# A hybrid recurrence step on one core: a limit on TensorE's instructions in time, joins in halves, small weights on ScalarE's queue, lent operand tiles as raw buffers

## The chip, the cores and the metric

The kernel runs on one core of a Trainium2 chip. The metric is the device time of one launch in microseconds, as the median of several runs.

## What is computed

One layer of a model that mixes two recurrences, for 128 context tokens and 512 sample tokens, all in float32 (D = 2048, FFN width 5632):

```python
h = rms_norm(x, L['norm_mix_pre']) * (1.0 + scale_m) + shift_m
proj = h @ L['w_in']                                  # 2048 x 5408
xl, gl, pr = jnp.split(proj, [LRU_WIDTH, 2 * LRU_WIDTH], axis=-1)
# RG-LRU, forward and backward: gates by 8 heads of 128x128, then a linear scan
lru_out = ((hs_f + hs_b) * jax.nn.gelu(gl)).astype(dt)
# RWKV-7, forward and backward, 16 heads of 64: S = S*w + (S @ -kk)(kk*a) + v k, y = S r
rwkv_out, wkv_fin = rwkv7(pr, shift_fn, wkv_S0, L)
out = jnp.concatenate([lru_out, rwkv_out], axis=-1) @ L['w_out']
x = x + gate_m * rms_norm(out, L['norm_mix_post'])
h = rms_norm(x, L['norm_ffn_pre']) * (1.0 + scale_f) + shift_f
gate, up = jnp.split(h @ L['ffn_w_gu'], 2, axis=-1)
x = x + gate_f * rms_norm((jax.nn.silu(gate) * up) @ L['ffn_w_down'], L['norm_ffn_post'])
```

The six shifts, scales and gates are 2048 wide each and come from `silu(c) @ w_mod + b_mod`.

## The kernel before

All 640 tokens lie in the free dimension, as two halves of 320; channels lie in the partitions, 128 a tile. A projection's weights arrive as raw tiles of 128x512 floats (256 KB) and are split into a high and a low part in a rounded format (`split`, tile w, six buffers); a product is then three full-width matmuls of the rounded kind for each half of the tokens (tile ps). The normalized input lies split in 16 pairs of tiles, hi0 to hi15 and lo0 to lo15. When the input projection `w_in` has read a pair for the last time, the pair is free until the mixer's result k is loaded back from DRAM (`mixd`) into pair k by `mix_load`.

The program text is not written in the order in which the engines run it. Each part of the work is a Python generator, a stream with a priority. The class `Sched` keeps a planned clock for each engine, knows a planned duration for each instruction and delay for each DMA, and takes, one after the other, the stream whose next instructions could start earliest (`run`). A stream that yields a list of instructions has them issued together. So the order on every engine is fixed when the program is built, and each engine works it off in that order; SyncE's queue of DMAs too. The planner's numbers change only this order.

Streams in the mixer, all at once: `loader` fetches raw weights, first of w_in, then of the output projection `w_out`, and mixes in raw tiles of `w_mod` (`mod_rate`); `main` multiplies (lowest priority, so it fills TensorE's idle time); `lru` does the RG-LRU for 8 pairs of heads, two directions each, with weights lruw; `gates` uses the same tile for the weights gup; `elem` prepares the 16 jobs (8 head pairs, two directions) of RWKV-7 with weights up; `inverse` and `join` invert each job's triangular 64x64 blocks; `chain` runs the recurrence over the chunks; `gn` normalizes and stores the result.

A `join` inverts by blocks: ten chunks, two heads. It sends 40 matmuls of 32x32 tiles from jt and af in one list, an evacuation by ScalarE into yj, 40 matmuls of 32x16 from yj, an update by VectorE, and then two lists of 20. A plain float32 matmul counts as two matmul records and two weight loads in the trace; the rounded kind as one of each.

The output projection comes in two passes over the 16 output tiles: the first (`EARLY`) takes the operand tiles 0 to 3 and 8 to 11 and goes on while the mixer still works; `evac_part` copies each partial sum into the only gt tile and stores it (`opd`). The second (`LATE`) takes the rest and adds the partial sums. Then follow the residual, which has VectorE busy, and the FFN, which keeps TensorE busy to the end.

Raw tiles come from one pool of four buffers (`self.raws`, `free_raw`) until the first pass is done. SyncE issues every DMA. In the profile nearly all compute instructions stand under line 127 and DMAs under line 121, in a helper that builds instructions; so tiles tell where one belongs. pa and pc are the accumulators of the mixer's small work.

Of the kernel before, what the change touches and what calls it, by code (L numbers as in the profile page):

```python
# [11 lines left out]
F32 = mybir.dt.float32  # L12
# [13 lines left out]
T = TP + TS  # L26
# [8 lines left out]
NC = 10  # L35
# [12 lines left out]
PATIENCE = 1.5  # L48
MODE, HOLD, HOLD_MOD = 0.35, 0.0, 8.0
LAT = {  # L50
    "pe": {"pe": 0.0, "act": 0.2, "dve": 0.2, "pool": 0.2, "sync": 0.15},
# [54 lines left out]
class Eng:  # L106
# [3 lines left out]
    def __getattr__(self, op):  # L110
        f, eng = getattr(self._r, op), self._n

        def make(*args, **kw):
# [3 lines left out]
            if op == "dma_start":  # L117
                n = 4
                for s in out.shape:
                    n *= s  # L120
                return Op(eng, lambda: f(*args, **kw), _box(out), [_box(x) for x in ins], 0.48, None, n)  # L121
            aset = None
# [62 lines left out]


class Sched:

# [5 lines left out]
    def __init__(self):  # L194
# [9 lines left out]
        self.now = 0.0  # L204
        self.win, self.busy, self.slow, self.parts, self.mode = 0, 0.0, True, [], True

    def own(self, tile_, res, t):
# [82 lines left out]
    def emit(self, op):  # L290
# [14 lines left out]
        if op.bytes:  # L305
            self.bus = max(e, self.bus) + op.bytes / 330e3
            e, eng = self.bus + 1.4, "dma"
            self.lane[self.ndma % 8] = e
            self.ndma += 1
# [53 lines left out]
    def run(self, until=None):  # L363
        while self.streams and not (until is not None and until in self.ev):
            best = None
            cand = []
            for st in self.streams:
# [13 lines left out]
                if ops[0].eng == "pe" and whole(ops[0]) != self.mode and (  # L381
                        self.mode is False or self.now - st[4] < (HOLD if st[0] < 8 else HOLD_MOD)):
                    s += MODE
                cand.append((s, st, ops))
                if best is None or s < best[0]:
# [8 lines left out]
            for op in best[2]:  # L394
                self.emit(op)
            self.step(best[1], None)
            self.poll()

    def fire(self, *names):
# [27 lines left out]
class Step:  # L427
# [223 lines left out]
    def free_raw(self):  # L651
        return next((r.take() for r in self.raws if r.slots), None)

# [172 lines left out]
    def loader(self):  # L826
# [41 lines left out]
        mk = [("m", k) for k in range(KT)]  # L868
        self.mod_rate = MOD_RATE2
        for m in range(KT):  # L870
            yield from self.rows(a["w_out"][m], self.evac_part(m), mk, EARLY)
# [33 lines left out]
    def lru(self):  # L905
        sc = self.sc
        for q in range(NPAIR):
# [5 lines left out]
            for d in range(2):  # L913
                r, av, i = yield self.take("u", 3)
                wt = yield self.take("lruw")
                yield self.q.dma_start(wt, self.a["lruw"][q, d])

# [62 lines left out]
    def elem(self):  # L980
        sc = self.sc
        for n in range(NJ):
# [7 lines left out]
            up = yield self.take("up")  # L990
            yield self.q.dma_start(up, self.a["lup"][p, d])
            sw, av, cs, pd = yield self.take("t", 4)
# [97 lines left out]
    def join(self, n):  # L1090
# [7 lines left out]
        for h in range(2):  # L1098
            for e in range(4):
                p0, c0 = 64 * h + 16 * e, 16 * (e % 2)  # L1100
                yield self.q.dma_start(got[p0:p0 + 16, :, c0:c0 + 16], self.xsc[p % 2][d][h, e].rearrange("c k i -> k c i"))
        yield self.v.transpose(out=turned, in_=got)
        Q = [slice(32 * q, 32 * q + 32) for q in range(4)]
        p3 = lambda t, w: t[:, 0:NC * w].rearrange("p (c t) -> p c t", t=w)
        ps = yield self.take("pa")
        yield [self.mm(ps[r, c * 32:(c + 1) * 32], af[r, c, 0, q // 2, 32 * (q % 2):32 * (q % 2) + 32], tq[r, c, :])
               for c in range(NC) for q, r in enumerate(Q)]
        yield self.copy(yy, p3(ps, 32))
        sc.rel(ps)
        o = slice(16, 32) if d == 0 else slice(0, 16)  # L1110
        ps = yield self.take("pa")
        yield [self.mm(ps[r, c * 16:(c + 1) * 16], yy[r, c, :], xd[r, c, o]) for c in range(NC) for r in Q]
        yield self.stt(xd[:, :, o], p3(ps, 16), self.rmask[:, d:d + 1], xd[:, :, o])
# [151 lines left out]
    def gates(self):  # L1265
# [3 lines left out]
        for p in range(NPAIR):  # L1269
            gw = yield self.take("lruw")  # L1270
            g1, g2 = gw[:, 0], gw[:, 1]
            yield self.q.dma_start(g1, self.a["gup1"][p])
            yield self.q.dma_start(g2[0:32], self.a["gup2"][p])
            g = yield self.take("gt")
# [56 lines left out]
    def evac_part(self, m):  # L1331
        def go(acc):
            t = yield self.take("gt")
            yield self.copy(self.v2(t), acc.v)
# [703 lines left out]
```

## Time and profile before

| | |
|---|---|
| three runs | 3404.69, 3408.0, 3411.7 us; median 3408.0 |
| profiled execution | 3410.4 us, span 3408.6 us |
| TensorE busy | 3213.6 us (94%), 25068 matmuls and as many weight loads |
| VectorE, ScalarE, GpSimd busy | 2205.9 us (65%), 1541.9 us (45%), 1465.0 us (43%) |
| stages | input norm to 100 us; mixer and input projection to about 1255 us; output projection to 1590 us; residual to 1700 us; FFN to the end |
| mean granted clock of TensorE | 0.966 |

All times are from one profiled execution. PE is TensorE, PEld its weight loads, DVE VectorE, ACT ScalarE, POOL GpSimd, SP SyncE; a small q stands for an engine's sequencer. A row of the windows view gives start and end, the length, the busy time of PE, PEld, DVE, ACT and POOL with the number of instructions, then the granted share of TensorE's clock (1.00 is 2.4 GHz, 0.50 is 1.2 GHz), the DMA engines' share and GB/s. A row of the waits view names who waited for whom, the total in us, how often, and the longest. A row of the timeline gives the start and the length in us of a group of instructions of one kind, what it writes and reads, how many, and in brackets the idle time before it with what ended it; "issue" is a wait that nothing in the profile explains.

### The profile page before, as it was taken

Reading aid. Unit: us, or ns where it says so; the run is one execution under the profiler, and the core shown is the slowest. Engines: PE = TensorE matmul, PEld = TensorE weight load, DVE = VectorE, ACT = ScalarE, POOL = GpSimd, SP = SyncE. Lnnn points to the kernel's source line nnn. Section 1 sums busy time; section 2 is a strip of 40 time slices with the busy share of each in tenths; the row PEclk is TensorE's granted clock in tenths of the full one; section 3 lists DMA queues with packets and bytes.
Section 4 is the critical chain, followed back from the end, with each engine's and each line's share of the span. In section 5 each row is a group of like instructions: output and inputs, shape, how many; then the busy total and the mean of one; then the engine's idle time right before and its main releaser. Section 6 shows DMA issues by size and latency. Waiting matters only on the chain.

```text
span 3408.6 us, 67001 instructions
## 1 busy us (share of the span) xinstructions
PE 3213.6 (94%) x25068; PEld 2892.3 (85%) x25068; DVE 2205.9 (65%) x3878; ACT 1541.9 (45%) x3282; POOL 1465.0 (43%) x1736
## 2 busy tenths in 40 slices
PE   6899999999999989897699999999999999999997
PEld 4787888888888877786499999999999988888885
DVE  4465667776776762267988888888888862323324
ACT  4435456665666656243444444444444432312223
POOL 1353345444544453256666666566666640000001
PEclk9999989999999999997799999999999999999998
DMA  9533334433333354685533333333333342423323
GB/s 382 173 100 93 98 91 115 111 97 110 99 91 109 104 162 145 205 277 173 176 103 95 103 103 98 96 101 102 91 106 100 101 147 77 136 77 105 97 77 133
DMA packets 262774, 422.55 MB, mean 124 GB/s; under 512 B 74801, under 2 KB 87729, under 8 KB 258353
## 3 DMA queue, kind: packets, MB, share of 16 engines
q1 hardware_dynamic: 262448, 418.27, 40.3%
q8 instruction: 198, 3.24, 0.4%
q14 instruction: 128, 1.04, 0.1%
HBM read 365.19 MB, written 52.96 MB: 123 GB/s over the span
## 4 chain that ended last, share of the span: by engine, by line
PE 80%; DVE 9%; DMA 6%; issue 2%; ACT 2%; SPq 1%; POOL 1%; DVEq 0%; POOLq 0%; ACTq 0%
PE pb L127 41%; PE ps L127 19%; PE pc L127 11%; PE pa L127 6%; DMA raw<-in_w_out_dram 2%; PE pm L127 2%; DVE pr L127 1%; DVE x L127 1%; DVE o L127 1%; SPq L121 1%; DVE lo L127 1%; DMA raw<-in_wmod_dram 1%; DVE xl L127 1%; DVE hi L127 1%; DVE u L127 1%
## 5 line engine op out<-in xcount | busy, mean ns | idle before, releaser
L127 PE MATMUL ps<-hi,w 128*128 128x320 f32 x3712 | 937.1, 330 | 34.4 <-POOL w L127 17.9
L127 PEld LDWEIGHTS ps<-hi,w 128*128 128x128 f32 x3712 | 649.3, 195 | 78.3 <-POOL w L127 26.7
L127 PE MATMUL ps<-lo,w 128*128 128x320 f32 x1856 | 600.5, 329 | 2.0 <-DVE lo L127 1.9
L127 POOL TENSOR_SCALAR w<-raw 128x256 fp32r<-128x256 f32 x403 | 196.4, 487 | 679.6 <-PE ps L127 475.6
L127 POOL TENSOR_TENSOR w<-raw,w 128x256 fp32r<-128x256 f32 x500 | 414.2, 830 | 159.8 <-PE ps L127 72.6
L127 POOL TENSOR_TENSOR hi<-raw 128x256 f32<-128x256 f32 (+1 forms) x307 | 291.6, 966 | 208.1 <-PE pb L127 188.4
L127 PEld LDWEIGHTS ps<-lo,w 128*128 128x128 f32 x1856 | 360.9, 194 | 18.9 <-issue 8.3
L127 ACT ACTIVATE w<-raw 128x256 fp32r<-128x256 f32 x421 | 173.7, 413 | 374.1 <-PE pb L127 259.7
L127 POOL TENSOR_TENSOR lo<-raw 128x256 f32<-128x256 f32 (+1 forms) x260 | 241.7, 943 | 171.6 <-PE pb L127 107.3
L127 PE MATMUL pb<-hi,lo 128*128 128x320 f32 (+1 forms) x984 | 292.4, 339 | 0.0
L127 DVE TENSOR_TENSOR w<-raw,w 128x256 fp32r<-128x256 f32 x324 | 187.0, 578 | 89.4 <-ACT w L127 77.5
L127 PE MATMUL pb<-hi,hi 128*128 128x320 f32 (+1 forms) x740 | 225.1, 340 | 0.6 <-DVE hi L127 0.6
L127 PE MATMUL pb<-lo,lo 128*128 128x512 f32 (+1 forms) x646 | 204.3, 356 | 0.0
L127 PEld LDWEIGHTS pb<-hi,lo 128*128 128x128 f32 x984 | 179.6, 189 | 13.3
L127 PE MATMUL pb<-lo,hi 128*128 128x320 f32 (+1 forms) x604 | 189.9, 346 | 0.0
L127 PE MATMUL pb<-x,lo 128*128 128x320 f32 x774 | 172.0, 310 | 2.7 <-DVE x L127 2.1
L127 PE MATMUL pb<-o,hi 128*128 128x320 f32 x726 | 173.8, 309 | 0.0
L127 PE MATMUL pb<-o,w 128*128 128x320 f32 x792 | 160.8, 311 | 0.4 <-DVE w L127 0.4
L127 DVE TENSOR_TENSOR lo<-raw 128x256 f32<-128x256 f32 (+1 forms) x268 | 157.3, 611 | 0.0
L127 PE MATMUL pb<-x,hi 128*128 128x320 f32 x590 | 154.5, 311 | 2.3 <-DVE hi L127 2.3
L127 ACT ACT_TABLE_LOAD x115 | 147.5, 1283 | 6.8 <-DMA st<-in_cT_dram 2.5
L127 DVE TENSOR_TENSOR hi<-raw 128x256 f32<-128x256 f32 (+1 forms) x221 | 145.6, 681 | 0.0
(395 smaller groups left out, 7504.7 us busy)
## 6 DMA issues: line engine op xcount, KB each, us to landing
raw<-in_w_gu_dram SPq DMA_DIRECT2D x352, 256.0 KB, 2.6
raw<-in_wmod_dram SPq DMA_DIRECT2D x256, 256.0 KB, 3.7
raw<-in_w_dn_dram SPq DMA_DIRECT2D x176, 256.0 KB, 2.6
raw<-in_w_in_dram SPq DMA_DIRECT2D x160, 256.0 KB, 3.4
mraw<-in_wmod_dram SPq DMA_DIRECT2D x32, 1024.0 KB, 8.8
raw<-in_w_out_dram SPq DMA_DIRECT2D x64, 256.0 KB, 4.3
gud<-z SPq DMA_DIRECT2D x44, 320.0 KB, 2.5
x<-in_xT_dram SPq DMA_DIRECT2D x32, 320.0 KB, 5.5
```

Source lines behind the costliest of these rows:

```text
L121: return Op(eng, lambda: f(*args, **kw), _box(out), [_box(x) for x in ins], 0.48, None, n)
L127: o = Op(eng, lambda: f(*args, **kw), _box(out), [_box(x) for x in ins], _cost(eng, op, out, ins), aset, 0)
```

## The change

The planner gets three new numbers. `AT_ONCE`, `FETCH` and `LATE_FETCH`: where TensorE's next list would bring the count of its instructions (two for a rounded matmul or a transpose, four for a plain one) within 2.6 us over 300, the list is planned 2.5 us later, so that another stream's work goes first. A DMA's planned landing is later by up to 1.0 us, by its size. A DMA issued by an engine other than SyncE is planned at 0.1 us of that engine. The first two lists of a join are yielded in two halves of 20. The loads of lruw, gup and up (48 in all) go from SyncE's queue (`self.q`) to ScalarE's (`self.s`). From the moment when the loader turns to w_out (`away`) until the last RG-LRU result is stored (`("mix", 7)`), `free_raw` may also take hi13 to hi15 and lo13 to lo15, six tiles more, and `evac_part` one of hi7, lo7, hi12 and lo12 instead of gt.

```diff
+FETCH, AT_ONCE, LATE_FETCH = 2.6, 300, 2.5
@@ Eng
-                return Op(eng, lambda: f(*args, **kw), _box(out), [_box(x) for x in ins], 0.48, None, n)
+                return Op(eng, lambda: f(*args, **kw), _box(out), [_box(x) for x in ins], 0.48 if eng == "sync" else 0.1, None, n)
...
+def count(ops):
+
+    return sum(2 if op.cost in (0.115, 0.147, 0.227) else 4 for op in ops)
@@ Sched.emit
-            e, eng = self.bus + 1.4, "dma"
+            e, eng = self.bus + 1.4 + min(1.0, op.bytes / 256e3), "dma"
@@ Sched.run
+                if ops[0].eng == "pe" and self.recent(s) + count(ops) > AT_ONCE:
+                    s += LATE_FETCH
...
+            if eng == "pe":
+                self.hist.append((self.now, count(best[2])))
...
+    def recent(self, t):
+
+        while self.hist and self.hist[0][0] < self.clk["pe"] - FETCH:
+            self.hist.popleft()
+        return sum(n for e, n in self.hist if e > t - FETCH)
@@ Step
     def free_raw(self):
-        return next((r.take() for r in self.raws if r.slots), None)
+        return next((r.take() for r in self.raws if r.slots), None) or self.lend(13, 14, 15, n=512)
+
+    def lend(self, *ks, n=T):
+
+        if "away" in self.sc.ev and ("mix", 7) not in self.sc.ev:
+            for k in ks:
+                for tag in ("hi%d" % k, "lo%d" % k):
+                    if self.R[tag].slots:
+                        return self.R[tag].take().bitcast(F32)[:, 0:n]
+        return None
@@ loader
         self.mod_rate = MOD_RATE2
+        self.sc.fire("away")
@@ lru
-                yield self.q.dma_start(wt, self.a["lruw"][q, d])
+                yield self.s.dma_start(wt, self.a["lruw"][q, d])
@@ elem
-            yield self.q.dma_start(up, self.a["lup"][p, d])
+            yield self.s.dma_start(up, self.a["lup"][p, d])
@@ join
+        halves = range(NC // 2), range(NC // 2, NC)
...
-        yield [self.mm(ps[r, c * 32:(c + 1) * 32], af[r, c, 0, q // 2, 32 * (q % 2):32 * (q % 2) + 32], tq[r, c, :])
-               for c in range(NC) for q, r in enumerate(Q)]
+        for cs in halves:
+            yield [self.mm(ps[r, c * 32:(c + 1) * 32], af[r, c, 0, q // 2, 32 * (q % 2):32 * (q % 2) + 32], tq[r, c, :])
+                   for c in cs for q, r in enumerate(Q)]
...
-        yield [self.mm(ps[r, c * 16:(c + 1) * 16], yy[r, c, :], xd[r, c, o]) for c in range(NC) for r in Q]
+        for cs in halves:
+            yield [self.mm(ps[r, c * 16:(c + 1) * 16], yy[r, c, :], xd[r, c, o]) for c in cs for r in Q]
@@ gates
-            yield self.q.dma_start(g1, self.a["gup1"][p])
-            yield self.q.dma_start(g2[0:32], self.a["gup2"][p])
+            yield self.s.dma_start(g1, self.a["gup1"][p])
+            yield self.s.dma_start(g2[0:32], self.a["gup2"][p])
@@ evac_part
-            t = yield self.take("gt")
+            t = yield lambda: self.lend(7, 12) or (self.R["gt"].take() if self.R["gt"].slots else None)
```

The order changes nearly everywhere, since one new number in the planner shifts all that follows. Three places show how.

TensorE at the seventh of the 16 joins, before: the first batch (jt,af), full-width matmuls of the input projection (ps), the second batch (jt,yj).

```order
L127 MATMUL pa<-jt,af 32x32 x40
L127 MATMUL ps<-hi_1165,w 128x320
L127 MATMUL ps<-lo_1166,w 128x320
L127 MATMUL ps<-hi_1165,w 128x320
L127 MATMUL ps<-lo_1166,w 128x320
L127 MATMUL ps<-hi_1165,w 128x320 x2
L127 MATMUL ps<-hi_1234,w 128x320
L127 MATMUL ps<-lo_1235,w 128x320
L127 MATMUL ps<-hi_1234,w 128x320
L127 MATMUL ps<-lo_1235,w 128x320
L127 MATMUL ps<-hi_1234,w 128x320
L127 MATMUL pa<-jt,yj 32x16 x40
```

The same join in the new order (pm are the modulation's matmuls):

```order
L128 MATMUL pa<-jt,af 32x32 x40
L128 MATMUL pm<-raw,scv 32x256 x4
L128 MATMUL ps<-hi_967,w 128x320
L128 MATMUL ps<-hi_1029,w 128x320
L128 MATMUL ps<-lo_1030,w 128x320
L128 MATMUL pa<-jt,yj 32x16 x20
L128 MATMUL ps<-hi_1029,w 128x320
L128 MATMUL pa<-jt,yj 32x16 x20
```

The first batch is still whole; the second is cut, with one full-width matmul between its halves, and eleven matmuls between the batches have become seven.

SyncE's queue around the second load of lruw, the one issued at 493.03 us, before: kd is the store of a k tile that waits to be computed.

```order
L121 DMA raw<-in_w_in_dram 128x512
L121 DMA raw<-in_wmod_dram 128x512
L121 DMA raw<-in_w_in_dram 128x512
L121 DMA kd_5132<-gt 128x640
L121 DMA lruw<-in_lruw_dram 128x256
```

ScalarE's queue around the first load of lruw in the new order, with what each row waits for (DMAHW are landings of earlier DMAs):

```order
L122 DMA up<-in_lup_dram 128x128 [waits DMAHW7_49]
L128 ACT_TABLE_LOAD
L128 ACTIVATE t<-pa,c_rp 128x320 [waits PE_49] x4
L128 ACTIVATE gt<-ps,c_lp 128x640 [waits DMAHW3_49,DVE_49]
L128 ACTIVATE yj<-pa 128x320 [waits PE_49]
L122 DMA lruw<-in_lruw_dram 128x256 [waits DMAHW6_49,DMAHW1_49]
L128 ACT_TABLE_LOAD
```

The load no longer stands behind raw tiles and the store; it stands behind ScalarE's evacuation of a join's batch, and what follows on ScalarE stands behind it. Of the 48 loads, 43 carry a wait of the DMAHW kind.

SyncE's queue in the first pass of the output projection, before:

```order
L121 DMA raw<-in_w_out_dram 128x512
L121 DMA opd_80<-gt 128x640
L121 DMA raw<-in_wmod_dram 128x512
L121 DMA out_o_wkv_dram<-yy 128x64
L121 DMA raw<-in_wmod_dram 128x512
L121 DMA raw<-in_w_out_dram 128x512
```

The same place in the new order:

```order
L122 DMA raw<-in_w_out_dram 128x512
L122 DMA raw<-in_wmod_dram 128x512 x2
L122 DMA hi_16658<-in_w_out_dram 128x512
L122 DMA hi_16664<-in_wmod_dram 128x512
L122 DMA opd_80<-hi_16682 128x640
L122 DMA out_o_wkv_dram<-yy 128x64
```

Weights now also land in hi and lo tiles, and the partial sum leaves from one.

## Rows read from the trace of the kernel before

**Rows 1.** Windows by stage: busy time of each engine, granted clock, DMA share:

```profile
100.00:1255.00 1155.00, 1095.69 (x11570) 960.94 (x11571) 777.27 (x1641) 666.24 (x1608) 542.81 (x760) 0.96 0.38 107
...
1700.00:3409.00 1709.00, 1678.02 (x10010) 1569.92 (x10008) 1132.77 (x1783) 637.18 (x1171) 698.79 (x719) 0.99 0.34 103
```

**Rows 2.** TensorE's own waits, 100 to 1255 us: total us, times, longest:

```profile
PE pa L127 <- issue: 12.0, 7, 3.0
...
PE pa L127 <- DMA lruw<-in_lruw_dram: 6.4, 4, 2.5
...
PE pa L127 <- DMA lruw<-in_gup_dram: 3.4, 4, 1.1
...
PE ps L127 <- issue: 2.1, 1, 2.1
...
PE pa L127 <- DMA up<-in_lup_dram: 1.4, 2, 0.7
```

**Rows 3.** Timeline of TensorE in three places with join batches:

```profile
423.74 0.41 PE L127 MATMUL ps<-hi,w 128*128 128x320 f32 x1
423.99 0.30 PE L127 MATMUL ps<-lo,w 128*128 128x320 f32 x1
424.13 0.46 PE L127 MATMUL ps<-hi,w 128*128 128x320 f32 x2
...
553.67 0.89 PE L127 MATMUL pa<-jt,af 32*32 32x32 f32 x80
...
556.66 0.97 PE L127 MATMUL pa<-jt,yj 32*32 32x16 f32 x80
...
845.93 0.92 PE L127 MATMUL pa<-jt,af 32*32 32x32 f32 x80
...
847.95 0.69 PE L127 MATMUL pa<-jt,yj 32*32 32x16 f32 x60
851.31 0.51 PE L127 MATMUL pa<-jt,yj 32*32 32x16 f32 x20 [2.67 <-issue]
```

**Rows 4.** DMA queues, 848.7 to 851.3 us: packets, MB, share of 16 engines:

```profile
q8 instruction: 1, 0.02, 2.3%
```

**Rows 5.** Windows over half-clock stretches, columns as in rows 1; sums last:

```profile
850.70:860.90 10.20, 9.59 (x87) 8.76 (x87) 5.89 (x10) 5.76 (x8) 2.43 (x3) 0.50 0.10 28
...
sum 27.10, PE 25.15 PEld 21.28 DVE 8.73 ACT 12.64 POOL 5.11; mean PE 8.38 PEld 7.09 DVE 2.91 ACT 4.21 POOL 1.70
...
sum 13.30, PE 13.30 PEld 11.78 DVE 2.54 ACT 8.19 POOL 3.46; mean PE 6.65 PEld 5.89 DVE 1.27 ACT 4.09 POOL 1.73
...
1355.90:1362.60 6.70, 5.36 (x16) 4.57 (x17) 1.06 (x1) 3.88 (x7) 2.97 (x5) 0.50 0.59 186
...
sum 23.60, PE 16.81 PEld 15.54 DVE 4.30 ACT 7.44 POOL 6.11; mean PE 4.20 PEld 3.89 DVE 1.07 ACT 1.86 POOL 1.53
```

**Rows 6.** Chain from 490 us; issues of lruw; SyncE's waits, 100 to 1440 us:

```profile
493.03 4.79 DMA lruw<-in_lruw_dram
...
L121 SPq DMA_DIRECT2D lruw<-in_lruw_dram x16: 422/432/1656, 431.0 to 1345.2; - x16
...
SPq L121 <- DMA xsc<-xl: 14.1, 10, 2.9
```

**Rows 7.** Waits of TensorE, 1245 to 1372 and 1372 to 1440 us, and GpSimd's:

```profile
PE ps L127 <- POOL w L127: 6.9, 5, 3.9
...
PE ps L127 <- POOL w L127: 8.2, 7, 4.1
...
POOL w L127 <- DMA raw<-in_w_out_dram: 94.0, 23, 8.9
```

**Rows 8.** Issues of stores and loads by tile: ns min/median/max, first, last start:

```profile
L121 SPq DMA_DIRECT2D mixd<-y x8: 319/324/433, 391.3 to 1383.4; - x8
L121 SPq DMA_DIRECT2D mixd<-lh x8: 319/323/382, 556.4 to 1371.8; - x8
...
L121 SPq DMA_DIRECT2D opd<-gt x16: 326/417/454, 1234.0 to 1430.3; - x16
```

More of the change, by code (lines that the diff above doesn't have):

```diff
@@ L205, in __init__ @@
         self.win, self.busy, self.slow, self.parts, self.mode = 0, 0.0, True, [], True
+        self.hist = deque()
     def own(self, tile_, res, t):
```

## The prediction

> **What bounds the kernel now.** I read the windows by stage first, then TensorE's own waits, then single places in the timeline, and last the chain and the waits of the queue that issues DMAs. In the mixer's stretch, 100 to 1255 us, TensorE is busy 1095.69 of 1155 us, and after 1700 us it is busy 1678.02 of 1709 [rows 1]. TensorE is the bound in both, and since the change neither adds nor removes a matmul, time can be won only where TensorE waits or runs at its lower clock. After 1700 us there is next to nothing to win. So the whole forecast lies in the mixer and in the first pass of the output projection behind it.
>
> Three causes of lost time can be named there.
>
> First, the joins. A join sends a batch of 40 tiny matmuls (160 TensorE instructions: the timeline counts 80 matmul records and there are as many weight loads), some full-width ones, and a second batch of 40. In [rows 3] a second batch stops after 60 of its 80 records for 2.67 us with "issue" as the cause: no semaphore ends that wait. In just those 2.6 us one packet of the queue "instruction" moved [rows 4]. So I read it as TensorE's sequencer running out of fetched instructions. The waits view has 12.0 us of it on pa in 7 waits and one of 2.1 us on ps [rows 2]: 14.1 us. The granted clock then falls to 0.50, which is 1.2 GHz, the lower of the two levels: 850.7 to 860.9 us is the stretch behind the stall of [rows 3], and three such stretches (the others 359.2 to 369.4 and 1041.9 to 1048.6 us) add up to 27.1 us [rows 5]. Half of that is lost: 13.6 us. The joins cost 14.1 + 13.6 = 27.7 us at most.
>
> Second, the small weights (lruw, up). TensorE waits for them 6.4 + 3.4 + 1.4 = 11.2 us [rows 2]. The load at 493.03 us takes 4.79 us until TensorE goes on, and SyncE, which issues it, spends 422 to 1656 ns on an issue [rows 6]; it had to get past a store of k that waited for its data. Two half-clock stretches follow such waits (499.2 to 509.3 and 1134.1 to 1137.3 us), 13.3 us [rows 5], half of it 6.7. Together 17.9 us.
>
> Third, the first pass of the output projection. Up to the last linear-recurrence result, stored at 1371.8 us [rows 8], TensorE waits 6.9 us for split weights, and another 8.2 us until 1440 us [rows 7]. GpSimd, which splits them, waited 94.0 us for the raw weights' transfers in the same stretch [rows 7]. So four raw buffers are too few there. Four half-clock stretches add 23.6 us [rows 5], of which 11.8 are lost; the second of them ends at 1362.6 us, and it and the first are 6.7 us long, so 6.7 is lost up to 1372 and 5.1 behind. So 13.6 us within reach of the lent buffers and 13.3 us behind them, 26.9 in all.
>
> **The change part by part.**
>
> *Joins.* In the new order of TensorE 9 of the 16 joins have one of their first two batches cut in two, and the number of other matmuls from the first batch to the end of the second has risen in the median from 6.5 to 9. What that is worth is read from distance: a second batch that starts 2.02 us behind the first stalls for 2.67 us, while one that starts 2.99 us behind, at 556.66 us, goes through without a break [rows 3]. Two and a half full-width matmuls at 0.14 us (423.99 to 424.13 us [rows 3]) are 0.35 us, about a third of the distance between those two cases. The limit is also soft, and 7 joins stay whole. So of the 27.7 us I take four tenths, 11.1 us; the bounds are nothing and all. Against it stands the price of the cuts. The first full-width matmul behind a batch holds the array for 0.25 us (423.74 to 423.99 us) where 0.14 is usual [rows 3], and I allow as much on entering: 0.2 us a cut, 9 cuts, 1.8 us. Net 9.3 us.
>
> *Small weights.* 48 loads leave SyncE, where they stood in one row with weight loads that wait for a free buffer, and now stand on ScalarE behind whatever it does. Their issue takes 48 times 0.43 us, the median of SyncE's [rows 6], some 21 us of ScalarE, which is busy only 666.24 of these 1155 us [rows 1]; as long as that cover holds the price is nothing. The planner now also reckons with a later landing, so TensorE's matmuls that need the weights stand further behind. Nothing in the trace shows a load issued by ScalarE. The gain lies between nothing and 17.9 us; I take six tenths, 10.7, since the place shown in the order has the load behind an evacuation that itself waits for a join.
>
> *Lent tiles.* Six idle operand halves become raw buffers from the end of the input projection's loads until 1371.8 us, in the old time. Four buffers gave waits of 13.6 us there; ten should take away two thirds of that, 9.1 us. Behind it only the head start helps: a fifth of 13.3, 2.7 us. 11.8 us; bounds nothing and 26.9. The staging tiles for the partial sums cost nothing and hide a store that no engine on the path waits for.
>
> *What is late next.* A shorter filler could meet the recurrence. The last of its results is stored at 1383.4 us, the last partial sum at 1430.3 us [rows 8]: 46.9 us of cover, more than the sum below. In the new order the last normalizing matmul stands 43 projection matmuls further back, about 6 us at 0.14; the cover holds.
>
> *The sum.* 9.3 + 10.7 + 11.8 = 31.8 us. The profiled execution took 3410.4 us, 1.8 more than its span, and the median of the timed runs is 2.4 lower. 3410.4 - 31.8 - 2.4 = **3376 us**.
>
> **A rule that speaks against it.** The trace shows instruction packets inside the stalls. By the Trainium skill, page "Runtime: NRT & Kernel Launch", section "Instruction fetch mechanics", an engine's sequencer fetches the next block of instructions by itself while it works on the current one, and the cost of a block's end is mostly hidden. By that rule a limit on instructions in time has nothing to win. The stop in the midst of a batch, where no operand is new, and the packet in it speak against the word "mostly" here.
>
> **The rivals.**
>
> *The joins are bound by something else.* The stalls stay and only the cuts are paid: 3410.4 + 1.8 - 10.7 - 11.8 - 2.4 = 3387 us. For it: "issue" is only the name for what the profile can't tell. Against it: the packets [rows 4]. That result is the one that the Trainium skill's rule above would give.
>
> *The change doesn't do what it says.* The limit lets through 300 instructions where a join alone has 320, so stalls merely move, and the lent buffers fill early without help, since a split also needs one of six tiles for its halves. Then only the small weights pay: 3410.4 + 1.8 - 10.7 - 2.4 = 3399 us. For it: the seventh join in the order stands closer together than before. Against it: GpSimd's 94.0 us [rows 7].
>
> *All of it goes.* 3410.4 + 1.8 - 27.7 - 17.9 - 26.9 - 2.4 = 3337 us. Against it: a new order brings waits of its own.
>
> *Slower: ScalarE is held up by its own loads.* Of the 48 loads 43 carry a wait for the landing of an earlier DMA. On SyncE such a wait for a small store took 14.1 us in 10 cases, 1.4 us each [rows 6]. On ScalarE everything queues behind it: the recurrence's copies (yy, svu), for which TensorE waits in a fixed order. 43 x 1.4 = 60 us of ScalarE. If three quarters reach TensorE, that is 45 against the 31.8 gained: 3410.4 - 31.8 + 45 - 2.4 = 3421 us. From 53% on the kernel is slower than before. Against it: ScalarE has 489 us to spare, and at issue most landings lie well back.
>
> **How the numbers follow.** About 0.2% (6.8 us) is what a measurement here can tell from no change: 3401 to 3415 us is "same". The forecast has 0.42 (3360 to 3390 us). The rule's rival has 0.08, "all of it" 0.10: both faster. "Doesn't do what it says" has 0.24, of which 0.14 below 3401, 0.09 within and 0.01 above. ScalarE's rival has 0.16: 0.15 slower and 0.01 within. So faster 0.42 + 0.08 + 0.10 + 0.14 = 0.74, same 0.10, slower 0.16. The range reaches from 3342, which leaves out half of "all of it" (0.05), to 3411, which leaves out ScalarE's rival (0.15).
>
> **What would show it.** Right: in TensorE's waits between 100 us and the end of the input projection "issue" on pa falls from 12.0 to about 7 us, and waits for lruw and up from 11.2 to under 5; half-clock stretches behind joins get fewer; between the end of the input projection and the last recurrence store TensorE waits under 3 us for split weights; the stretch from the residual on keeps its length. Wrong: "issue" stays or moves to other tiles; ScalarE's waits grow around its loads and TensorE's waits for ScalarE with them; the first pass waits for GpSimd itself rather than for transfers. If the last part grows in length, the cause lies in a part of the order that I took as unchanged.

## The result

| | before | after |
|---|---|---|
| median of the runs | 3406.35 us (3400.58 to 3411.7) | 3356.6 us (3342.8 to 3366.87) |
| ratio, 95% interval | | 0.9852 [0.9809, 0.9894] |
| profiled execution, span | 3410.4, 3408.6 us | 3366.87, 3364.9 us |

The kernel became 50 us faster by the medians, 36 to 65 us by the interval. The forecast was 3376 us in a range of 3342 to 3411. The profiled execution of after is the slowest of its four, so its span shows 43.7 of the 50 us.

To see where they went I cut the execution at two points that every version has: SyncE's first issue of a w_out load and its last issue of opd. In each part I add up TensorE's **lost time** from its records: the gaps in which it neither multiplies nor loads weights, plus, for each stretch at the lower clock, its length times one minus the granted clock. The span less all lost time is 3097.0 us before and 3096.7 after (the first 100 us and the 24.2 us behind TensorE's last instruction counted as lost too, 24.2 in both). So lost time tells the difference where the lengths of the parts do not, since TensorE's work moves between them.

| lost time, us (idle + clock) | before | after | difference | predicted |
|---|---|---|---|---|
| mixer, from 100 us to the first w_out load | 51.4 + 41.0 = 92.4 | 46.0 + 32.4 = 78.4 | -14.0 | -20.0 |
| first pass, to the last opd | 27.8 + 17.1 = 44.9 | 6.9 + 10.2 = 17.1 | -27.8 | -11.8 |
| all behind it | 59.5 + 58.0 = 117.5 | 54.8 + 59.1 = 113.9 | -3.6 | 0 |

**The mixer.** TensorE's waits after, from 100 to 1255 us (who waited for whom; total us, times, longest), beside [rows 2]:

```profile
PE pc L128 <- DVE svu L128: 8.6, 13, 2.7
...
PE pc L128 <- issue: 5.1, 2, 2.7
...
PE pa L128 <- issue: 3.2, 5, 0.9
...
PE pa L128 <- DMA up<-in_lup_dram: 1.4, 4, 0.4
...
PE ps L128 <- issue: 1.0, 1, 1.0
...
PE pa L128 <- DMA lruw<-in_lruw_dram: 0.5, 1, 0.5
```

The small weights are nearly gone from the list: 1.4 + 0.5 = 1.9 us instead of 11.2. Their issue on ScalarE's queue (columns as in [rows 6]):

```profile
L122 ACTq DMA_DIRECT2D lruw<-in_lruw_dram x16: 334/335/364, 430.1 to 1329.3; - x16
```

"Issue" on pa fell from 12.0 to 3.2 us, but pc now has 5.1 us that it did not have; with ps the sum went from 14.1 to 9.3 us. One of the two pc stalls in the timeline of TensorE (start, length in us, idle time in brackets):

```profile
776.67 0.53 PE L128 MATMUL pa<-jt,yj 32*32 32x16 f32 x40
777.12 0.80 PE L128 MATMUL pc<-af,svu 128*64 128x64 f32 x20
777.86 0.79 PE L128 MATMUL pc<-ar,sa 64*64 64x64 f32 x18
781.36 0.47 PE L128 MATMUL pc<-ar,sa 64*64 64x64 f32 x2 [2.72 <-issue]
```

The join's half stands directly ahead of the recurrence's own two batches of 20 records each. The third batch stops after 18 of 20 for 2.72 us, as the join's did in [rows 3]. The queue "instruction" from 778.6 to 781.4 us (packets, MB, share of the engines), and the window from the end of the stall (columns as in [rows 1]):

```profile
q8 instruction: 1, 0.02, 2.2%
```

```profile
781.13:787.96 6.83, 6.60 (x130) 5.07 (x132) 3.01 (x6) 0.98 (x2) 0.00 (x0) 0.50 0.69 201
```

Again one packet, and then 6.83 us at half clock. So the same kind of stall came back at another batch, one that now follows directly on the cut join's half.

**The first pass.** The windows from the first w_out load to the last opd, before and then after:

```profile
1186.50:1430.30 243.80, 215.80 (x2053) 183.49 (x2052) 100.03 (x189) 129.03 (x287) 96.15 (x128) 0.93 0.54 160
```

```profile
1172.00:1391.10 219.10, 211.95 (x2091) 186.79 (x2092) 104.98 (x194) 120.27 (x274) 107.66 (x156) 0.95 0.60 182
```

About the same number of matmuls in 219.10 us instead of 243.80, with 182 GB/s instead of 160. The waits that have to do with the split weights w, in these windows, before:

```profile
POOL w L127 <- DMA raw<-in_w_out_dram: 89.5, 22, 8.9
...
PE ps L127 <- POOL w L127: 15.2, 12, 4.1
```

and after:

```profile
POOL w L128 <- PE ps L128: 81.5, 70, 5.4
...
POOL w L128 <- DMA raw<-in_w_out_dram: 3.4, 1, 3.4
```

GpSimd's wait for raw weights fell from 89.5 to 3.4 us. It now waits 81.5 us for TensorE to free a split tile, so the order of who waits has turned round, and TensorE's matmuls have no row for GpSimd's w left. The stores of the last partial sums (ns, first and last start), beside [rows 8]:

```profile
L122 SPq DMA_DIRECT2D mixd<-y x8: 326/380/624, 393.0 to 1368.6; - x8
```

```profile
L122 SPq DMA_DIRECT2D opd<-hi x12: 319/326/431, 1229.9 to 1358.4; - x12
L122 SPq DMA_DIRECT2D opd<-gt x4: 320/320/382, 1365.3 to 1391.1; - x4
```

From the last mixd<-y to the last opd there were 46.9 us of cover; now 22.5 are left (1391.1 - 1368.6).

### The profile page after: what moved, and what is told of

Read it like the earlier page. It is cut to its first block, busy times and chain, and to the rows that moved or that the text cites. A ratio compares the mean times of both kernels' runs of the same rounds, so it can differ in the third digit from the quotient of the medians.

```text
span 3364.9 us, 66999 instructions
## 1 busy us (share of the span) xinstructions
PE 3200.5 (95%) x25068; PEld 2888.0 (86%) x25068; DVE 2211.7 (66%) x3872; ACT 1532.3 (46%) x3265; POOL 1475.9 (44%) x1762
## 4 chain that ended last, share of the span: by engine, by line
PE 82%; DVE 9%; DMA 4%; ACT 2%; issue 2%; SPq 1%; POOL 1%; DVEq 0%; ACTq 0%; POOLq 0%
PE pb L128 43%; PE ps L128 20%; PE pc L128 12%; PE pa L128 6%; PE pm L128 2%; DVE pr L128 1%; DVE x L128 1%; DVE o L128 1%; DVE xl L128 1%; DVE bk L128 1%; DVE lo L128 1%; SPq L122 1%; DVE svu L128 1%; DMA raw<-in_w_in_dram 1%; DVE z L128 0%
## 5 line engine op out<-in xcount | busy, mean ns | idle before, releaser
L128 PE MATMUL ps<-hi,w 128*128 128x320 f32 x3712 | 919.7, 326 | 19.4 <-ACT hi L128 8.5
L128 POOL TENSOR_TENSOR w<-raw,w 128x256 fp32r<-128x256 f32 x469 | 388.7, 829 | 138.6 <-PE ps L128 56.5
L128 PEld LDWEIGHTS ps<-lo,w 128*128 128x128 f32 x1856 | 355.9, 192 | 20.5 <-issue 9.8
L128 PE MATMUL pb<-lo,lo 128*128 128x320 f32 (+1 forms) x932 | 282.5, 340 | 0.1
L128 PE MATMUL pb<-lo,hi 128*128 128x320 f32 (+1 forms) x695 | 211.2, 344 | 0.2 <-DVE lo L128 0.2
L128 DVE TENSOR_TENSOR hi<-raw,lo 128x512 fp32r<-128x512 f32 x88 | 60.9, 692 | 213.5 <-ACT lo L128 185.8
L128 PE MATMUL pb<-x,hi 128*128 128x320 f32 x936 | 197.7, 311 | 0.0
L128 DVE TENSOR_TENSOR lo<-raw,hi 128x512 fp32r<-128x512 f32 x85 | 58.9, 693 | 200.0 <-ACT hi L128 162.0
L128 PEld LDWEIGHTS pb<-lo,lo 128*128 128x128 f32 x932 | 167.8, 188 | 13.6 <-DVE z L128 0.3
L128 DVE TENSOR_TENSOR hi<-raw 128x128 f32<-128x128 f32 (+1 forms) x228 | 159.0, 712 | 0.0
L128 PEld LDWEIGHTS pb<-x,hi 128*128 128x128 f32 x936 | 154.2, 190 | 0.0
```

The source lines that it names most:

```text
L128: o = Op(eng, lambda: f(*args, **kw), _box(out), [_box(x) for x in ins], _cost(eng, op, out, ins), aset, 0)
```

## The experiments

Twelve more kernels were measured, in three groups of four, each group on one chip. A ratio stands against runs of before from the same group (medians 3400.72, 3399.65 and 3409.6 us); it is taken over the runs and is not the quotient of the two medians. "Bursts" counts TensorE's stalls of over 0.4 us, 100 to 1400 us, whose matmul has no releaser and that begin behind 250 or more TensorE instructions in 5 us.

| kernel | us | ratio [95%] | lost: mixer | first pass | behind | bursts |
|---|---|---|---|---|---|---|
| before | | 1 | 92.4 | 44.9 | 117.5 | 8, 14.9 us |
| lend_only | 3368.2 | 0.9887 [0.986, 0.9915] | 81.1 | 18.3 | 109.0 | 9, 17.9 |
| limit_only | 3386.29 | 0.994 [0.9919, 0.9961] | 56.4 | 41.8 | 109.7 | 3, 5.2 |
| weights_only | 3408.75 | 1.0017 [0.9996, 1.0038] | 97.6 | 50.0 | 105.1 | 3, 4.2 |
| landing_only | 3391.99 | 0.9976 [0.9956, 0.9996] | 78.0 | 47.8 | 111.3 | 8, 9.1 |
| after | 3356.6 | 0.9852 [0.9809, 0.9894] | 78.4 | 17.1 | 113.9 | 7, 9.0 |
| after_no_lend | 3378.56 | 0.9935 [0.9914, 0.9956] | 68.9 | 40.0 | 111.6 | 5, 5.5 |
| after_no_limit | 3371.35 | 0.9906 [0.9878, 0.9935] | 82.8 | 27.1 | 107.0 | 4, 5.8 |
| after_weights_sync | 3404.49 | 1.0012 [0.9997, 1.0026] | 122.5 | 21.1 | 106.8 | 2, 3.0 |
| after_no_landing | 3383.14 | 0.9941 [0.992, 0.9962] | 87.3 | 22.0 | 112.9 | 2, 3.0 |
| queue_before | 3398.64 | 0.997 [0.9953, 0.9987] | 77.5 | 46.0 | 117.7 | 9, 14.5 |
| queue_after | 3352.98 | 0.9848 [0.9817, 0.9878] | 77.9 | 12.8 | 115.2 | 7, 8.7 |
| shuffle_after | 3351.39 | 0.984 [0.9816, 0.9863] | 61.8 | 25.1 | 103.0 | 4, 8.3 |
| window5 | 3341.41 | 0.9809 [0.9792, 0.9827] | 54.4 | 4.2 | 106.6 | 0 |

The lost times are of one profiled execution each. How far those scatter shows in three kernels whose order on TensorE is the same to the row up to the loader's turn to w_out: before, lend_only and queue_before have 92.4, 81.1 and 77.5 us in the mixer. So differences of some 15 us there can be the execution and not the kernel. The same holds for a single wait: TensorE waits 11.2 us for lruw, gup and up in before and 4.2 + 1.6 + 1.2 = 7.0 in lend_only, where these loads stand as they stood. The span less all lost time lies between 3094.8 and 3103.1 us, except in limit_only (3114.0) and window5 (3113.4). The first theories were these. "First pass": the lent tiles are most of the gain. "Fetch": the limit ends the stalls at joins. "Truer order": the later planned landing removes the waits for small weights. "Shuffle": each new order moves the time either way, and the parts do not add up.

### The lent tiles: alone, and taken out

lend_only is the kernel before with these lines; after_no_lend is after without them:

```diff
-        return next((r.take() for r in self.raws if r.slots), None)
+        return next((r.take() for r in self.raws if r.slots), None) or self.lend(13, 14, 15, n=512)
+        self.sc.fire("away")
-            t = yield self.take("gt")
+            t = yield lambda: self.lend(7, 12) or (self.R["gt"].take() if self.R["gt"].slots else None)
```

> The kernel before with the lent tiles alone (six operand tiles as raw buffers, four as staging tiles in the first pass of the output projection). Theory 'first pass': TensorE's waits for split weights there (15.1 us) and the half-clock stretches behind them (11.8 us lost) are most of the 50 us that the change won; so about 25 us faster than before, 3381 us, and the last partial sum stored some 25 us earlier behind an unchanged mixer. Theory 'fetch': most was won at the joins; then this run is within 10 us of before. Theory 'shuffle': each new order moves the time by some 10 to 15 us either way and the parts don't add up.

> The changed kernel without the lent tiles. Theory 'first pass': it loses about 25 us, 3381 us, and the waits for split weights between the end of the input projection and the last partial sum are back at 10 us or more. Theory 'fetch' or 'shuffle': it loses under 10 us.

Alone the tiles give 0.9887 [0.986, 0.9915], some 38 us (32.5 by the medians); without them 28 us of the gain are missing (0.9935 - 0.9852 = 0.0083 of 3400). In the first pass of after_no_lend the waits are back: GpSimd waits 88.1 us for raw weights of w_out, and TensorE 15.9 for split ones. The window of lend_only from the first w_out load to the last opd:

```profile
1178.90:1388.70 209.80, 199.80 (x2034) 175.71 (x2035) 101.54 (x188) 120.91 (x263) 108.44 (x150) 0.96 0.61 186
```

The 243.80 us of before have become 209.80. Over all kernels the column "first pass" falls into two groups: 40.0 to 50.0 us lost without the lent tiles, 4.2 to 27.1 with them, and no kernel lies between. "First pass" stands. It is the one part of the change that the profile separates cleanly from the order.

### The limit: alone, and taken out

```diff
+                if ops[0].eng == "pe" and self.recent(s) + count(ops) > AT_ONCE:
+                    s += LATE_FETCH
+        for cs in halves:
```

> The kernel before with the limit of 300 instructions in 2.6 us and the joins in halves alone. Theory 'fetch': 20 us or more faster than before, and the waits named issue on pa fall from 12.0 us to under 5. Theory 'first pass': the stalls move to other batches instead of going, time within 10 us of before, issue on pa, pc and ps together still over 10 us. Theory 'shuffle': anything within 15 us of before with no match between issue and time.

> The changed kernel without the limit on instructions in time and with whole joins. Theory 'fetch': it loses 20 us or more and issue on pa is back at 10 us or more. Theory 'first pass': it loses under 10 us, since the trace of the changed kernel still has about 14 us of such stalls.

The limit and the halves alone give 0.994 [0.9919, 0.9961], and taking them out of after costs 18 us by the same reckoning. In limit_only "issue" is 5.5 us on pa and 1.2 on pc, where theory 'fetch' had under 5 on pa. But the stalls do not follow the limit. The three kernels with the order of before in the mixer (before, lend_only, queue_before) have 14.5 to 17.9 us of them. Of the other orders, the three without the limit (weights_only, landing_only, after_no_limit) have 4.2 to 9.1 us, and those with the limit of 2.6 us have 3.0 to 9.0. So what these show is that the order of before was a bad one for such stalls and that the others have fewer. The limit as built is not shown to be the cause.

### The small weights: alone, and back on SyncE

weights_only moves the 48 loads and lowers their planned cost. after_weights_sync has them back on SyncE, in the plan too:

```diff
-                yield self.s.dma_start(wt, self.a["lruw"][q, d])
+                yield self.q.dma_start(wt, self.a["lruw"][q, d])
```

> The kernel before with the loads of lruw, gup and up issued by ScalarE alone (planned at 0.1 us of ScalarE). My prediction's term: 10.7 us faster than before; TensorE's waits for lruw and up fall from 11.2 us to under 5. Rival: the issuing engine doesn't matter, since the planner still reckons with a landing that comes too early; then these waits stay over 8 us and the time is within 5 us of before. Second rival: ScalarE is held up, 10 us slower or more, with TensorE's waits for ScalarE grown by as much.

> The changed kernel with the small weights back on SyncE's queue. My prediction's term: it loses about 10 us, and waits of TensorE for lruw and up are back at 6 us or more. Rival: the later planned landing does the work, not the queue; then it loses under 5 us and these waits stay under 4 us.

Both went against expectation. weights_only gained nothing, though it waits only 1.3 + 0.7 = 2.0 us for up and lruw. after_weights_sync lost all that the whole change gives, while its waits for the same loads are short too. TensorE's waits in it, 100 to 1255 us:

```profile
PE pc L128 <- DVE svu L128: 20.1, 18, 3.9
PE pa L128 <- DVE jt L128: 8.5, 8, 2.6
...
PE pa L128 <- DMA up<-in_lup_dram: 1.2, 2, 0.7
PE pa L128 <- DMA lruw<-in_gup_dram: 1.2, 2, 1.0
```

The weights cost 2.4 us, but the recurrence's svu 20.1 where after has 8.6, and 122.5 us are lost in the mixer. Such waits can come from where TensorE's dependent matmuls stand. That needed a test in which the order stays.

### The same order, the other queue

Here the planner sees the loads where it saw them, and only the engine that issues them is the other one. TensorE's order is the same (in queue_before to the row; in queue_after the weight loads to the row and the matmuls but for 4 of 25068 records). In queue_after:

```diff
+        self.sq = Eng("act", n.sync)
-                yield self.s.dma_start(wt, self.a["lruw"][q, d])
+                yield self.sq.dma_start(wt, self.a["lruw"][q, d])
```

queue_before has the mirror, `Eng("sync", n.scalar)`, in the kernel before.

> The changed kernel with one physical difference: the 48 loads of lruw, gup and up are issued by SyncE at the places in the program that the planner chose for ScalarE, so the order of TensorE and all other compute is the same to the row. The theory queue says that the place on SyncE's queue itself costs: these loads stand behind stores and raw loads again, TensorE's waits for lruw, gup and up rise from 2 us to over 10, and most of the 54 us by which the kernel with the weights planned on SyncE was slower comes back: 3385 to 3410 us. The theory shuffle says that those 54 us were the other order and not the queue: within 10 us of the changed kernel, 3345 to 3367 us.

> The mirror of it: the kernel before, its order of compute unchanged to the row, with the 48 loads issued by ScalarE. The prediction's term for the small weights is 10.7 us (at most 17.9: waits of 11.2 us and half-clock stretches worth 6.7), and the rival in which ScalarE is held up gives a loss of 45. The theory shuffle (that the order made the difference in the runs with a new planner) leaves room for the term, since here nothing else moves: if the queue was the cause of the waits, lruw and gup fall from 9.8 us to under 3 and the time to about 3390 us (0.997). If the loads were late because they are asked for late, the waits stay and the time is the same.

queue_after is as fast as after. TensorE waits more for the loads:

```profile
PE pa L128 <- DMA up<-in_lup_dram: 3.0, 4, 1.2
...
PE pa L128 <- DMA lruw<-in_gup_dram: 2.7, 1, 2.7
PE pa L128 <- DMA lruw<-in_lruw_dram: 2.6, 2, 1.5
```

8.3 us instead of 1.9, and yet nothing shows in the time: the mixer loses 77.9 us against 78.4. So the 54 us by which after_weights_sync falls behind after belong to the order that the planner made, and not to the queue.

In the order of before the queue does pay: 0.997 [0.9953, 0.9987], 4 to 16 us. The waits and the issues of lruw in queue_before:

```profile
PE pa L127 <- DMA up<-in_lup_dram: 3.1, 2, 1.8
PE pa L127 <- DMA lruw<-in_gup_dram: 1.1, 1, 1.1
...
PE pa L127 <- DMA lruw<-in_lruw_dram: 0.5, 1, 0.5
```

```profile
L121 ACTq DMA_DIRECT2D lruw<-in_lruw_dram x16: 334/334/369, 427.2 to 1333.8; - x16
```

11.2 us of waits have become 4.7, and the longest of these issues of lruw is 369 ns where SyncE's was 1656 [rows 6]. Part of the 6.5 us can be the execution, as the 7.0 us of lend_only show. The waits view does not list the waits of ScalarE's queue. By the records each of the 48 issues begins, but for under 0.1 us in all, no later than the end of ScalarE's work ahead of it, so none was held up by a landing.

By the Trainium skill, page "DMA: Bandwidth & Descriptors", section "Issuing engines are not separate DMA queues", another issuing engine saves only the sequencer's time for the issue, which is usually small. queue_after agrees, with 0.9848 against 0.9852. queue_before shows a gain of 4 to 16 us; whether SyncE's saved issue time or the loads' place in its queue gives it, no run tells apart.

### The planned landing: alone, and taken out

```diff
-            e, eng = self.bus + 1.4, "dma"
+            e, eng = self.bus + 1.4 + min(1.0, op.bytes / 256e3), "dma"
```

> The kernel before with the later planned landing of DMAs alone (up to 1.0 us by size). The prediction gave this part no price of its own. Theory 'truer order': an order that reckons with later landings has TensorE wait less for lruw and up (11.2 us before, then under 6) and for split weights, so 10 us or more faster than before. Rival: without more buffers and without another queue the data comes no earlier, so the time is within 5 us of before.

> The changed kernel with the old planned landing of DMAs. Theory 'truer order': it loses 10 us or more and TensorE's waits for lruw and up, nearly gone in the changed kernel, are back at 5 us or more although ScalarE issues these loads. Rival: it loses under 5 us.

Alone it is worth 0 to 4 parts in a thousand, though it cuts the waits for lruw, gup and up from 11.2 to 4.9 us. Without it after loses 30 us by the ratios, of which the profiled executions show 16.4 (spans of 3381.3 and 3364.9): 8.9 as lost time in the mixer and 4.9 in the first pass. The waits for lruw, gup and up did not come back with it: after_no_landing has 1.0 us of them, where theory 'truer order' had 5 or more. So that theory fails on its own sign. Whether the term or the order that it happened to give is the cause, these two runs do not tell.

### A control

```diff
-PATIENCE = 1.5
+PATIENCE = 1.45
```

> A control: the changed kernel with a number of the planner that has nothing to do with the change moved by a hair (PATIENCE, by which ScalarE's table switches are put off, from 1.5 to 1.45 us). The order shifts nearly everywhere. The theory shuffle says that such a hair is worth 10 to 40 us by itself, and that most runs that took one part out of the changed kernel show as much of this as of the part: 3365 to 3395 us. The theory that each part pays what its removal cost (28, 18, 54, 30 us) says that nothing is lost here: 3345 to 3367 us.

The order changes in thousands of rows and the time does not: 0.984. So a new order need not cost anything, and "shuffle", as I put it, falls for this one push. What is left is a weaker statement: after_weights_sync and queue_after together show that an order can cost 54 us, the control that a small push to the planner need not. What makes the order of after_weights_sync so much worse is open; its waits for svu are where it shows.

### A limit over a longer time

By the records the stalls come behind 254 to 430 instructions in 5 us in before and 281 to 361 in after (the one at 778.65 us behind 345). In 2.6 us there were at most 279 and 222, and 163 at 778.65 us, so a limit of 300 in 2.6 us does not see them.

```diff
-FETCH, AT_ONCE, LATE_FETCH = 2.6, 300, 2.5
+FETCH, AT_ONCE, LATE_FETCH = 5.0, 260, 5.0
```

> The changed kernel with a limit that looks at what the stalls show: they come behind 320 to 350 instructions in 5 us, and the packet that ends them lands shortly before TensorE goes on. Here the limit is 260 instructions in a planned 5.0 us (instead of 300 in 2.6), with a delay of 5.0 us; by the durations of the trace no stretch of 5 us in the order holds more than 320 any more, where the changed kernel has 25 such stretches. The theory fetch says that stalls without a cause behind 250 or more instructions in 5 us (9.7 us in 8 places in the changed kernel, 23.7 in 12 before) fall to under 3 us, and the time falls or stays within the shuffle. If the stalls depend on where the program's blocks of instructions end and not on the rate, they stay at 4 to 10 us.

The 23.7 and 9.7 us of this expectation also count five stalls, 8.8 us in before and 0.7 in after, in which only the weight load has no releaser and the matmul behind it waits for gt, jt or lruw. Without these it is 14.9 us in 8 places and 9.0 in 7.

The bursts are gone, all of them, and it is the fastest kernel here: 3341.41 us, and each of its four runs (3337.76 to 3342.66) is below every run of queue_after and shuffle_after on the same chip (lowest 3345.57). The 0 in the table follows from the column's definition alone, since by the records no 5 us of window5 hold more than 237 instructions (432 in before, 375 in after, 100 to 1400 us). What counts is that TensorE's waits, 100 to 1255 us, have no row "issue" at all; these are left of the rows that [rows 2] shows:

```profile
PE pa L128 <- DMA lruw<-in_lruw_dram: 1.6, 2, 1.1
PE pa L128 <- DMA up<-in_lup_dram: 0.8, 2, 0.6
PE pa L128 <- DMA lruw<-in_gup_dram: 0.4, 1, 0.4
```

The windows of the mixer, after first, then window5:

```profile
100.00:1255.00 1155.00, 1102.83 (x11690) 963.48 (x11686) 790.28 (x1648) 681.81 (x1651) 539.19 (x754) 0.97 0.40 112
```

```profile
100.00:1255.00 1155.00, 1110.30 (x11819) 964.69 (x11820) 793.37 (x1625) 712.48 (x1653) 557.23 (x773) 0.99 0.41 117
```

The granted clock is 0.97 in after and 0.99 in window5. From 100 us to the last opd 13.7 us are lost to the clock (all in the mixer), where after loses 42.6. Of these 42.6, the four half-clock stretches that begin during such a stall or within 5 us of its end (at 272.5, 644.6, 781.1 and 921.1 us) lose 20.5; before the second of them stands a wait of 2.6 us for jt as well. The other 22.1 stand behind other waits. Three of the seven stalls, the one of 2.40 us at 1056.2 us among them, have no such stretch behind them.

Not all of it is gained: lost time over the whole execution is 45.6 us less than in after, the span 28.9 us. (The two profiled executions are the slowest of after and the fastest of window5; the medians differ by 15.2 us. And 7.3 of the 45.6 us lie behind the first pass, where shuffle_after has as little.) The 16.7 us between them are time in which TensorE counts as busy; more changes between small and full-width tiles, which hold the array longer [rows 3], would do that, but no run takes this price by itself. One join of it in the timeline:

```profile
556.12 0.80 PE L128 MATMUL pc<-af,svu 128*64 128x64 f32 x20
556.85 0.80 PE L128 MATMUL pc<-ar,sa 64*64 64x64 f32 x20
557.58 0.53 PE L128 MATMUL pa<-jt,yj 32*32 32x16 f32 x40
558.03 0.56 PE L128 MATMUL ps<-hi,w 128*128 128x320 f32 x2
```

The same three kinds of batches in a row as at 777 us in after, the join's half last here, without a stop: the join's second half comes at 563.94 us, 6.4 us later, and the first batch of the join lies 7 us ahead of this half (550.51).

The records of all kernels settle what these stalls are. Besides window5, thirteen kernels have 75 stalls of over 0.4 us whose matmul has no releaser (100 to 1400 us). Each of the 75 ends 1.23 to 1.60 us behind the end of the last packet on the queue "instruction" that carries TensorE's packets (q8); of the 613 other gaps of that length in all kernels only 26 do. In before this queue moves 92 packets from 100 to 1255 us for 23141 TensorE instructions, one for about 250.

So "fetch" stands as a mechanism: TensorE goes on when a packet of instructions has come, and the one order with at most 237 instructions in any 5 us has no such stall. A safe rate is not shown, since 4 of the 75 stand behind only 223 to 241 instructions in 5 us. Nor does a second order show that this limit, and not another trait of the one order, makes window5 the fastest kernel.

By the Trainium skill, page "Runtime: NRT & Kernel Launch", section "Instruction fetch mechanics", the cost of crossing into the next block of instructions is mostly hidden. Here 14.9 us of stalls in before and 9.0 in after were not hidden.

## Why the prediction was right

The time lies inside the range, 19 us below the forecast of 3376 and just outside the band of 3360 to 3390 us that the forecast itself was given. The sum had 31.8 us; the profiled span fell by 43.7 and the median by 50. Its parts were off in opposite directions, the first pass gained 16 us more than its term and the mixer 6 less than its two, and that the one in part makes up for the other is luck. How the gain outside the first pass divides among the limit, the queue and the planned landing, the runs do not show.

- **What bounds the kernel.** Right. TensorE's lost time before the end of the first pass was the place; the lost time behind it fell by 3.6 us only, and that part's length from 1978.3 to 1973.8 us.
- **Lent tiles, -11.8, measured -27.8 in the first pass** (26.6 in lend_only, 22.9 between after_no_lend and after). This is the term that was mis-sized. The mechanism was right: GpSimd's wait for raw weights went from 89.5 to 3.4 us, and the forecast of under 3 us for split weights was met with none. The step that failed was to cut the 26.9 us twice, by a third for waits that would stay, and by four fifths behind 1372 us, where "only the head start helps". The head start was enough. About the whole upper bound was paid: the trace already showed who waited for whom in a chain, raw, split, matmul, and with the first link mended GpSimd has time to spare, 81.5 us of waits for TensorE.
- **Joins, -9.3, and small weights, -10.7: together -14.0 measured in the mixer.** The waits moved as forecast (issue on pa to 3.2 where I said 7, the small weights to 1.9 where I said under 5), but "issue" came back on pc with 5.1 us, which the text named as a sign that it would be wrong. The step that failed is the one that took the join alone as the burst: two of the seven stalls in after stand in the recurrence's batches of 20 records. The clock's half of the term did not come: half-clock stretches behind such stalls lose 20.5 us in before (five stretches) and 20.5 in after (four). And since one execution of the same order can differ by 15 us in the mixer, 14.0 is not told apart from 20.0.
- **The small weights' queue.** In the old order its price was right, 10.7 against a measured 4 to 16 us. The 11.2 us of waits behind it were high for that order, 7.0 in lend_only. In the new order the queue is worth nothing (queue_after): the waits rise from 1.9 to 8.3 us and the time does not. Why those waits cost nothing there is not shown.
- **The rivals.** ScalarE was not held up: its 48 issues in after begin 0.1 us in all behind the end of its work ahead of them, and the gain in queue_before has the other sign. "The joins are bound by something else" is refuted by the packets at the end of all 75 stalls and by window5. "Doesn't do what it says" was half right for the limit, which left stalls of 9.0 us.
- **The cover.** I said it would hold, and it did, though 22.5 of 46.9 us are left. That is because the first pass gained more than its forecast.

## What to carry to other kernels

If an engine's stall has no releaser and a packet of instructions lands shortly before its end, count the instructions of the last several us, over all batches and not one batch alone, and spread them; see that the limit's time is as long as what you saw ahead of the stalls. Where one term is a chain of waits with spare time in every other link, take its upper bound and not a fraction. With a planner that reorders everything, test a part by changing the hardware side and keeping the planned order, or the reshuffle will be read as the part.

## What was not expected of the hardware

- TensorE's stalls without a releaser end 1.23 to 1.60 us behind the end of an instruction packet, in 75 of 75 cases. They are gone in the one order that holds at most 237 TensorE instructions in any 5 us by the records, where before has up to 432 and after up to 375. Single batches of 160 instructions still run without a stop.
- A stretch at half clock stands behind some of these stalls and not behind others. In after four of the seven have one, and these stretches lose 20.5 us with 4.9 us of stalls. Over the kernels the clock does not follow the stalls: after_weights_sync has 3.0 us of them and loses 63.1 us to the clock in the mixer and the first pass.
- The issue of a load of in_lruw takes ScalarE 334 ns at the median and no more than 369 in queue_before, where SyncE took up to 1656 [rows 6]; over all 48 loads ScalarE's longest is 468 ns.
